# Attention on one core, part of the exponentials on VectorE: the fixed point put into PSUM, a twelfth group for VectorE, and three middle passes on GpSimd

## The chip, the cores and the metric

The kernel runs on one core of a Trainium2 chip. A core has five engines that run side by side, each through its own list of instructions in order, with semaphores between them: TensorE (PE in the profile; its weight loads are PEld), VectorE (DVE), ScalarE (ACT), GpSimd (POOL) and SyncE (SP), which here issues DMAs. SBUF is the working memory of 128 partitions, PSUM the memory that TensorE writes its products to. The metric is the device time of one execution in microseconds (us). Before the change it is 117.99 us, the median of three runs (117.93 to 118.18).

## The reference

```python
def setup_inputs():
    batch, heads, seq, dim = 8, 8, 512, 64
    return {
        "q": np.random.randn(batch, heads, seq, dim).astype(np.float32),
        ...
    }

def reference(q, k, v):
    scale = 1.0 / np.sqrt(q.shape[-1])
    scores = np.einsum('bhqd,bhkd->bhqk', q, k) * scale
    scores = scores - scores.max(axis=-1, keepdims=True)
    attn = np.exp(scores)
    attn = attn / attn.sum(axis=-1, keepdims=True)
    return np.einsum('bhqk,bhkd->bhqd', attn, v).astype(np.float32)
```

This is attention for 64 heads, each of 512 positions of 64 numbers. The kernel leaves out the subtraction of the maximum, which cancels in the quotient.

## The kernel before

The 64 heads are worked off as 32 pairs. For each pair, SyncE loads q, k and v (256 KB each); GpSimd rounds them to 16 bits (`cast`, lines L446 and L456); TensorE transposes q and k into PSUM (`transposes`, L480) and VectorE copies the result to SBUF (`copy`, L493). Then TensorE computes the scores, keys along the partitions. Two blocks of 128 keys by 512 queries make a group of 128 x 1,024 scores that fills one score buffer (tile `st`, L522); there are four groups in a pair, 128 in all, and the very last is done in two halves. A pool of three score buffers is used in strict rotation: group m takes the buffer of group m - 3.

ScalarE takes the exponential of a whole group in one instruction (`pt`, L527) and writes it to SBUF as 16-bit numbers. TensorE then multiplies these weights with v (`values`, L604). v carries an extra column of ones, so that the sum of the weights comes out with the product. VectorE takes the reciprocal of that sum (L582) and multiplies it in (`normalise`, L584), and SyncE stores the finished heads.

Eleven of the groups do not go to ScalarE. They are listed in `ON_DVE`, and VectorE computes their exponential by arithmetic on the bits of a number. TensorE first puts a constant into the score buffer (the `lift` matmuls, L508) and adds the scores. Then VectorE makes four instructions over 1,024 columns: the raise (`raise_`, L544) reads PSUM, multiplies the scores by `STEP` and writes `z`, a number whose upper bits are the exponent and whose lower 16 bits are the fraction. Then come three passes (`pass_`, L561) for a polynomial of that fraction: the first reads the fraction from `z` twice and writes `y`, the middle pass reads `y` twice, and the last reads `y` and `z` and writes the weights `pd`. For the last group of the list (`SHARED = 1`) GpSimd makes the middle pass in two instructions (`middle`, L574 and L577).

The order of all this is fixed before the kernel is built, by the class `Plan`. It steps through time in 5 ns steps with a cost for every kind of instruction (`EXP`, `COPY`, `NORM`, `RAISE`, `PASS`, `CAST`, `MIDDLE`), and decides at each step what TensorE, VectorE, GpSimd and SyncE do next. VectorE prefers copies that the next scores need, then raises, then other work that is ready (`step_dve`); a pass is only started where nothing of more urgency falls due before its end, with tolerances `LATE_NORM` and `LATE_COPY`. The planner keeps `port`, a time until which GpSimd and VectorE's passes exclude each other. `free` tells when the next score buffer can be written, `emit` releases a GpSimd cast, and from the time `CALM` on, each cast is made to wait for the VectorE instruction named last before it (`cast_behind`). Every engine then runs its list in that order, and only semaphores decide the times. The steps `raise`, `pass`, `middle`, `scores` and `last` are those that the change touches, besides the start (`first_pair`), where the first pair is rounded, transposed and scored ahead of the planned part.

Of the kernel before, what the change touches and what calls it, by code (L numbers as in the profile page):

```python
# [17 lines left out]
class Plan:  # L18
# [6 lines left out]
    COPY, NORM, RAISE = (601, 690), (307, 390), (1132, 1215)  # L25
    COPY_1 = (400, 190)
    NORM_COLUMN, PASS_DONE = 67, 80
    PASS, PASSES = 1131, 3
# [3 lines left out]
    CALM, KEEN = 14000, 6  # L32
    FIRST_UNIT = 4
    ON_DVE = (7, 20, 28, 40, 51, 56, 70, 80, 84, 98, 112)
    SHARED = 1

    LATE_NORM, LATE_COPY, HURRY, SOON, BACKLOG = 1000, 2200, 900, 80, 1200
# [7 lines left out]
    def __init__(self, groups, pairs, first):  # L45
# [4 lines left out]
        self.read = []  # L50
        self.exps = {}
        for m in range(first):
            self.act += self.EXP + self.EXP_FIXED
            self.exps[m] = self.act + self.EXP_DONE
            self.read.append(self.exps[m])
# [90 lines left out]

    def free(self, n=0):
        m = self.m + n
        if m >= len(self.groups):
            return 1e9  # L150
        g = self.groups[m][0][0]
        return max(0 if m < 3 else self.read[m - 3], self.tq.get(g, 1e9))
# [4 lines left out]
    def scores(self, t):  # L157
        m, grp = self.m, self.groups[self.m]
        half = m >= len(self.groups) - 2
        slots = 2 if 0 < grp[0][0] and grp[0][2] == grp[1][2] and not half else 1  # L160
        on_dve = self.for_dve(m)
        self.note(t, "scores", m, on_dve)
        t += (0 if self.tiled else self.INTO) + self.SLOT * slots
        self.tiled = True
        if on_dve:
            t += self.OFFSET
            self.ready.append((t + self.TO_DVE, "raise", (m,)))
            self.read.append(1e9)
        else:
            begin = max(self.act, t + self.TO_ACT)  # L170
            self.idle = getattr(self, "idle", 0) + begin - self.act
            self.act = begin + self.EXP // (2 if half else 1) + self.EXP_FIXED
            self.exps[m] = self.act + self.EXP_DONE
            self.read.append(self.exps[m])
        self.m += 1
        self.pe = t
# [35 lines left out]
    def last_values(self, t):  # L212
        g, h = self.last
        if self.m < len(self.groups) or self.last_part == 4:
            return False
        if t < max(self.wants(g, h, self.last_part), self.read[self.last_part // 2 - 3]):
            return False
        self.note(t, "last", self.last_part)
        self.full(t, self.V_UNIT)
        if self.last_part % 2:  # L220
            self.ready.append((self.pe + self.TO_DVE, "finish", (self.last_part // 2,)))
        self.last_part += 1
        return True
# [58 lines left out]
    def step_dve(self, t):  # L282
# [8 lines left out]
        if now:  # L291
# [3 lines left out]
            _, kind, what = job  # L295
            slots = 2 if kind == "raise" else 1
# [7 lines left out]
            if kind == "norm":  # L304
                more = self.NORM_COLUMN * what[1]
                self.dve = t + self.NORM[0] + more
# [5 lines left out]
            elif kind == "copy":  # L312
                held, done = self.COPY if what[0] != 1 else self.COPY_1
                self.dve = t + held
                self.banks[what[1]] = self.tq[what[0]] = t + done + self.TO_PE
            else:
                self.dve = t + self.RAISE[0]
                self.read[what[0]] = t + self.RAISE[1] + self.TO_PE
                self.passes += [(what[0], s, 0) for s in range(self.PASSES)]
            self.dve_done = self.dve  # L320
        elif any(x[2] <= t for x in self.passes):
            m, s, _ = job = next(x for x in self.passes if x[2] <= t)
            end = max(t, self.port) + self.PASS
            late = {"copy": self.LATE_COPY, "norm": self.LATE_NORM, "raise": self.LATE_NORM, "finish": 0}
            if all(x[0] > end - late[x[1]] for x in self.ready):
                self.passes.remove(job)
                self.note(t, "pass", m, s)
                self.dve = self.port = self.dve_done = end
                if s == 0 and m in self.ON_DVE[len(self.ON_DVE) - self.SHARED :]:
                    self.passes.remove((m, 1, 0))  # L330
                    self.passes[self.passes.index((m, 2, 0))] = (m, 2, 1e9)
                    self.casts.append(("middle", m, end + self.TO_POOL))
                    self.note(end, "middle", m)
                if s == self.PASSES - 1:
# [19 lines left out]
def kernel(  # L354
# [12 lines left out]
    scale = float(D) ** -0.5  # L367
    NP = (B * H) // 2
# [22 lines left out]
    ps_st = ctx.enter_context(tc.tile_pool(name="ps_st", bufs=3, space=bass.MemoryType.PSUM))  # L391
# [18 lines left out]
    heads = []  # L410
    raised = {}
# [29 lines left out]

    def cast(g, name):
# [10 lines left out]
        if (g, name) == (1, "q"):  # L453
            nc.vector.tensor_copy(out=dst[:, :, 0:2], in_=src[:, :, 0:2])
            return nc.gpsimd.tensor_copy(out=dst[:, :, 2:4], in_=src[:, :, 2:4])
        return nc.gpsimd.tensor_copy(out=dst, in_=src[:, :, :, :])  # L456
# [41 lines left out]
    def scores(m, on_dve):  # L498
# [3 lines left out]
        st = ps_st.tile([P, 2, S], FP32, tag="st", name=f"st_{m}")  # L502
# [21 lines left out]
        if on_dve:  # L524
# [3 lines left out]
            out=pt[:, :, cols], in_=st[:, :, cols], func=EXP, scale=scale  # L528
# [8 lines left out]
    LIFT, STEP = (793.0 / 32, -0.039907195352 / 32), scale * 1.4426950408889634 * 1024  # L537
    QUARTIC = (7.77974906 * 2.0**16, -8.78105033 * 2.0**32, 4.4655924e-3 * 1024 * 2.0**-64)

    def raise_(m):  # L540
# [6 lines left out]
                scalar1=STEP,  # L547
                scalar2=2.0**17,
                op0=AluOp.mult,
                op1=AluOp.max,  # L550
# [3 lines left out]
    def pass_(m, s):  # L554
        r = raised[m]
        f = r["z"].bitcast(U16).rearrange("p x (s n) -> p x s n", n=2)[:, :, :, 0]
        if s == 0:
# [5 lines left out]
                in0=r["y"][:, :, :] if s else f,  # L563
# [14 lines left out]

    def normalise(u, n):
        o, x = os[u // 7], u % 7  # L580
        rc = opool.tile([P, 7, 1], FP32, tag="rc", name=f"rc_{u}")
        nc.vector.reciprocal(out=rc[:, 0:n], in_=o[:, x : x + n, D : D + 1])  # L582
# [29 lines left out]
    def last_values(part):  # L612
        half, second = divmod(part, 2)
        if not second:
            o = ps_st.tile([P, 2, S], FP32, tag="st", name=f"o_last{half}")
# [39 lines left out]
    def first_pair():  # L655
# [8 lines left out]
        def twice(h, i, n):  # L664
            return tq[:, h, i : i + n].rearrange("p i (x d) -> p i x d", x=1).broadcast_to([P, n, 2, D])

        nc.vector.tensor_copy(out=q16[:, 0, 0:2], in_=twice(0, 0, 2))
        nc.vector.tensor_copy(out=k16[:, 0, 0:2], in_=tk[:, 0, 0:2])
        nc.scalar.copy(q16[:, 0, 2:4], twice(0, 2, 2))
        nc.gpsimd.tensor_copy(out=k16[:, 0, 2:4], in_=tk[:, 0, 2:4])  # L670
        nc.scalar.copy(k16[:, 1], tk[:, 1])
        nc.gpsimd.tensor_copy(out=q16[:, 1], in_=twice(1, 0, NI))

        st0, pka, st1 = (
            ps_st.tile([P, 2, S], FP32, tag="st", name=f"st_{n}") for n in ("0a", "ka", "1")
        )
# [16 lines left out]
        def first_scores(st, h, j, q0, q1, pt, s0, s1):  # L693
            for x in range(2):
# [9 lines left out]
                out=pt[:, :, q0:q1], in_=st[:, :, s0:s1], func=EXP, scale=scale  # L704
# [23 lines left out]
        st0b = ps_st.tile([P, 2, S], FP32, tag="st", name="st_0b")  # L728
# [9 lines left out]
        st2 = ps_st.tile([P, 2, S], FP32, tag="st", name="st_2")  # L738
# [5 lines left out]
    with tc.manual_schedule():  # L744
# [7 lines left out]
        for p in (32, 96):  # L752
            nc.vector.memset(lift[p : p + 32], LIFT[1])
        for n in range(NV):
# [13 lines left out]
            "finish": finish,  # L768
            "norm": lambda u, n, b: normalise(u, n),
        }  # L770
# [32 lines left out]
```

## Time and profile before

| what | us |
|---|---|
| median of three runs | 117.99 |
| lowest, highest | 117.93, 118.18 |
| the profiled execution | 117.88 |
| its span in the trace | 116.1 |

The profile is one execution on the chip. Its page gives each engine's busy time and share of the span; groups of instructions by source line, with the tile written and the tiles read (`pt<-st`), their count, their busy time, the mean duration of one, and the idle time of the engine just ahead of them with what ended it; and the chain of work that ended last. The trace behind it gives windows (busy time of each engine in a stretch) and timelines (instructions in order: start, duration, engine, line). A duration in a timeline runs until the result has landed, so that consecutive instructions of an engine can overlap by about 0.1 us. TensorE's clock was granted in full throughout (0.992 on average), and the DMA engines moved 33.83 MB at 291 GB/s.

### The profile page before, as it was taken

The page shows a single profiled execution, that of the slowest core. Times are in us where ns is not written, and L with a number is a line of the kernel's source. Part 1 is how long each engine was busy: PE and PEld are TensorE (multiplying, and loading weights), DVE is VectorE, ACT ScalarE, POOL GpSimd, SP SyncE. Part 2 cuts the span into 40 slices and gives each one's busy share as a digit, 9 for nine tenths or more (in the row PEclk, how much of TensorE's full clock was granted, in tenths as well). Part 3 has the DMA queues.
Part 4 walks back from the last instruction along what each step waited for, and adds up shares of the span by engine and source line. Part 5 has one row for each costly group of instructions (what it writes and reads, how often), then busy time and mean ns, then how long its engine had stood idle before and what let it go on. Part 6 is the DMA issues. An engine that isn't in the chain of part 4 may idle for free.

```text
span 116.1 us, 4085 instructions
## 1 busy us (share of the span) xinstructions
PE 104.8 (90%) x1581; PEld 66.9 (58%) x1581; DVE 101.4 (87%) x177; ACT 109.7 (95%) x122; POOL 60.5 (52%) x104
## 2 busy tenths in 40 slices
PE   7979989989999999999799979999989999999980
PEld 2635557546676466646465646467845567576660
DVE  3455997699999999999999999999999999969381
ACT  4599999999999999999999999999999999999980
POOL 2378519954653655555425546954484255596000
PEclk9999999999999999999999999999999999999996
DMA  3999999999999999999999999999999994222354
GB/s 109 286 372 380 384 378 384 388 375 375 344 323 319 307 293 336 311 338 307 352 307 305 321 328 241 296 376 324 329 292 358 366 291 167 93 93 93 101 184 133
DMA packets 35604, 33.83 MB, mean 291 GB/s; under 512 B 2688, under 2 KB 35584, under 8 KB 35584
## 3 DMA queue, kind: packets, MB, share of 16 engines
q1 hardware_dynamic: 35152, 33.24, 87.1%
q10 hardware_dynamic: 432, 0.33, 0.9%
q8 instruction: 12, 0.20, 0.7%
q14 instruction: 8, 0.07, 0.2%
HBM read 25.17 MB, written 8.39 MB: 289 GB/s over the span
## 4 chain that ended last, share of the span: by engine, by line
ACT 31%; DVE 30%; PE 18%; DMA 10%; issue 7%; POOL 1%; SPq 0%; POOLq 0%; ACTq 0%
ACT pt L527 29%; DVE y L561 7%; DVE tqk L493 6%; DMA k<-in_k_dram 6%; DVE z L544 6%; PE st L522 6%; PE o L604 6%; DVE ring L584 5%; DMA v<-in_v_dram 4%; DVE pd L561 4%; PE st_0a L653 3%; ACT pt L703 2%; PE tp L480 2%; POOL qkp L456 1%; DVE rc L582 1%
## 5 line engine op out<-in xcount | busy, mean ns | idle before, releaser
L527 ACT ACTIVATE pt<-st 128x1024 f16<-128x1024 f32 (+1 forms) x115 | 104.8, 1216 | 0.0
L522 PE MATMUL st<-tqk 64*128 64x512 f16 (+1 forms) x250 | 44.6, 380 | 4.3 <-ACT pt L527 3.1
L604 PE MATMUL o<-vp,pt 128*128 128x65 f16 x920 | 43.0, 194 | 1.4 <-DVE tqk L493 0.9
L604 PEld LDWEIGHTS <-pt 128*128 128x128 f16 x920 | 36.3, 98 | 11.0 <-issue 9.7
L446 POOL CAST vp<-v 128x512 f16<-128x512 f32 x32 | 19.6, 616 | 18.6 <-DVE y L561 10.9
L456 POOL CAST qkp<-k 128x512 f16<-128x512 f32 x31 | 19.0, 613 | 14.1 <-PE st L522 4.7
L584 DVE TENSOR_TENSOR ring<-o,rc 128x448 f32<-128x448 f32 (+2 forms) x37 | 22.6, 612 | 1.3
L456 POOL CAST qkp<-q 128x512 f16<-128x512 f32 x30 | 18.4, 613 | 10.1 <-DVE y L561 4.8
L522 PEld LDWEIGHTS <-tqk 64*128 64x128 f16 x250 | 13.1, 93 | 17.6 <-issue 10.1
L493 DVE COPY tqk<-tp 128x1024 f16<-128x1024 f16 x30 | 20.3, 683 | 2.3 <-PE tp L480 2.2
L480 PE MATMUL tp<-ident,qkp 128*128 128x128 f16 x248 | 20.5, 220 | 0.6 <-DVE tqk L493 0.2
L480 PEld LDWEIGHTS <-qkp 128*128 128x128 f16 x248 | 14.2, 97 | 8.8 <-issue 4.8
L561 DVE SCALAR_TENSOR_TENSOR pd<-y,z 128x1024 uint32<-128x1024 f32 x11 | 14.2, 1288 | 0.0
L544 DVE TENSOR_SCALAR z<-st 128x1024 f32<-128x1024 f32 x11 | 13.4, 1217 | 0.9 <-PE st L522 0.9
L561 DVE SCALAR_TENSOR_TENSOR y<-z 128x1024 f32<-128x1024 uint16 x11 | 13.9, 1261 | 0.1
L604 PE MATMUL o<-vp,pd 128*128 128x65 f16 x88 | 13.1, 194 | 0.3 <-DVE pd L561 0.2
L561 DVE SCALAR_TENSOR_TENSOR y<-y 128x1024 f32<-128x1024 f32 x10 | 12.3, 1234 | 0.0
L604 PEld LDWEIGHTS <-pd 128*128 128x128 f16 x88 | 8.6, 98 | 3.2 <-issue 2.4
L582 DVE RECIPROCAL rc<-o 128x7 f32<-128x7 f32 (+2 forms) x37 | 7.3, 196 | 3.3 <-PE o L604 3.2
L508 PE MATMUL st<-const-bfloat16-1.0,lift 64*128 64x512 bf16 x22 | 4.3, 381 | 0.4 <-ACT pt L527 0.4
L653 PE MATMUL st_0a<-const-bfloat16-1.0 128*128 128x512 bf16 (+1 forms) x11 | 3.5, 482 | 0.8 <-PEq L787 0.8
L653 PEld LDWEIGHTS <-const-bfloat16-1.0 128*128 128x128 bf16 x15 | 1.7, 129 | 2.5 <-issue 2.4
(50 smaller groups left out, 25.0 us busy)
## 6 DMA issues: line engine op xcount, KB each, us to landing
out_dram<-ring SPq DMA_DIRECT2D x63, 128.0 KB, 3.8
k<-in_k_dram SPq DMA_DIRECT2D x31, 256.0 KB, 5.1
q<-in_q_dram SPq DMA_DIRECT2D x31, 256.0 KB, 5.0
v<-in_v_dram SPq DMA_DIRECT2D x27, 256.0 KB, 5.2
v<-in_v_dram SPq DMA_DIRECT2D x10, 128.0 KB, 4.1
k<-in_k_dram ACTq DMA_DIRECT2D x2, 128.0 KB, 2.9
q<-in_q_dram SPq DMA_DIRECT2D x2, 128.0 KB, 2.7
out_dram<-obl SPq DMA_DIRECT2D x1, 64.0 KB, 1.6
```

What stands on the lines that cost most here:

```text
L446: return nc.gpsimd.tensor_copy(out=vps[g % NV][:, :, :, 0:D], in_=raw[g]["v"][:, :, :, :])
L456: return nc.gpsimd.tensor_copy(out=dst, in_=src[:, :, :, :])
L480: nc.tensor.transpose(tps[g][:, n, i, :], qkp[g][:, n, i, :], ident)
L493: nc.vector.tensor_copy(out=tqk[g][:, :, :], in_=tps.pop(g).rearrange("p n i c -> p n (i c)"))
L522: nc.tensor.matmul(st[:, x, cols], kc, qc[:, cols], start=not on_dve, stop=True)
L527: nc.scalar.activation(out=pt[:, :, cols], in_=st[:, :, cols], func=EXP, scale=scale)
L544: nc.vector.tensor_scalar(out=r["z"][:, :, :], in0=r["st"][:, :, :], scalar1=STEP, scalar2=2.0**17, op0=AluOp.mult, op1=AluOp.max,)
L561: nc.vector.scalar_tensor_tensor(out=r["bits"][:, :, :] if last else r["y"][:, :, :], in0=r["y"][:, :, :] if s else f, scalar=QUARTIC[s], ...
L582: nc.vector.reciprocal(out=rc[:, 0:n], in_=o[:, x : x + n, D : D + 1])
L584: nc.vector.tensor_tensor(out=ring[:, u % NU : u % NU + n, :], in0=o[:, x : x + n, 0:D], in1=rc[:, 0:n].broadcast_to([P, n, D]), op=AluOp. ...
L604: nc.tensor.matmul(os[u // 7][:, u % 7, :], blocks[(g, c, h)][:, y * P : (y + 1) * P], vps[g % NV][:, h, c, :], start=(c == 0), stop=(c == ...
L653: nc.tensor.matmul(dst[:, 0:n], ones[:, 0:P], ones[:, 0:n], start=True, stop=True)
```

## The change

Four things change together.

1. The factor `STEP` is no longer multiplied in by the raise. k is multiplied by 16 and q by `STEP / 16` when they are rounded to 16 bits, so that the score buffer in PSUM holds the fixed-point number itself. The rounding instructions of q and k become multiplications by a constant (`times`), on GpSimd and, in the first pairs, on VectorE and ScalarE. ScalarE's exponentials take `scale / STEP`. The constant that `lift` adds becomes 143 * 1024 - 3/64 per head. The raise keeps only its maximum.
2. The first pass reads the low 16 bits from the score buffer in PSUM and the clamped fraction from `z`, where it read `z` twice. The score buffer is given back after the first pass, not after the raise.
3. The three score buffers become three tiles with a tag each, and the planner takes the one that is free earliest (`pick`), in place of the rotation.
4. `ON_DVE` has twelve groups at other places, and `SHARED` names three of them, 57, 72 and 105, whose middle pass GpSimd makes. The planner's times and tolerances are others; a pass may not start before 117 ns after the one that it depends on; the first pass does not count for `port`, and up to two casts may be released ahead of it. A step that makes the reciprocal apart (`recip`, `mult`) is added and switched off (`APART = False`).

```diff
-    COPY, NORM, RAISE = (601, 690), (307, 390), (1132, 1215)
+    COPY, NORM, RAISE = (601, 690), (307, 390), 1132
...
+    RECIP, RECIP_DONE, CHAINED = 80, 230, 117
+    APART, ROOM = False, 0
...
-    CALM, KEEN = 14000, 6
+    CALM, KEEN = 20000, 6
...
-    ON_DVE = (7, 20, 28, 40, 51, 56, 70, 80, 84, 98, 112)
-    SHARED = 1
-
-    LATE_NORM, LATE_COPY, HURRY, SOON, BACKLOG = 1000, 2200, 900, 80, 1200
+    ON_DVE = (7, 13, 26, 36, 47, 57, 63, 72, 80, 93, 105, 110)
+    SHARED = (57, 72, 105)
+
+    LATE_NORM, LATE_MULT, LATE_COPY, HURRY, SOON, BACKLOG = 1600, 1300, 1400, 800, 80, 1500
...
+    def pick(self):
+        return min(range(3), key=lambda b: self.buffers[b])
+
     def free(self, n=0):
...
-        return max(0 if m < 3 else self.read[m - 3], self.tq.get(g, 1e9))
+        return max(sorted(self.buffers)[n], self.tq.get(g, 1e9))
...
-                self.dve = t + self.RAISE[0]
-                self.read[what[0]] = t + self.RAISE[1] + self.TO_PE
-                self.passes += [(what[0], s, 0) for s in range(self.PASSES)]
+                self.dve = t + self.RAISE
+                self.passes += [(what[0], s, 1e9 if s else self.dve + self.CHAINED) for s in range(self.PASSES)]
...
-            end = max(t, self.port) + self.PASS
+            end = (max(t, self.port) if s else t) + self.PASS
...
+                if s:
+                    self.port = end
+                else:
+                    self.buffers[self.buffer[m]] = end + self.PASS_DONE + self.TO_PE
...
+    STEP = scale * 1.4426950408889634 * 1024
+    TIMES = {"k": 16.0, "q": STEP / 16.0}
...
-    ps_st = ctx.enter_context(tc.tile_pool(name="ps_st", bufs=3, space=bass.MemoryType.PSUM))
+    ps_st = ctx.enter_context(tc.tile_pool(name="ps_st", bufs=1, space=bass.MemoryType.PSUM))
...
+    def times(engine, out, x, name):
+        return engine.tensor_scalar(
+            out=out, in0=x, scalar1=TIMES[name], scalar2=None, op0=AluOp.mult
+        )
...
-        return nc.gpsimd.tensor_copy(out=dst, in_=src[:, :, :, :])
+        return times(nc.gpsimd, dst, src[:, :, :, :], name)
...
+    def buffer(b, name):
+        return ps_st.tile([P, 2, S], FP32, tag=f"st{b}", name=name)
...
-            out=pt[:, :, cols], in_=st[:, :, cols], func=EXP, scale=scale
+            out=pt[:, :, cols], in_=st[:, :, cols], func=EXP, scale=scale / STEP
...
-    LIFT, STEP = (793.0 / 32, -0.039907195352 / 32), scale * 1.4426950408889634 * 1024
+    LIFT = (143.0 * 1024 / 32, 0.0, -3.0 / 64)
...
                 in0=r["st"][:, :, :],
-                scalar1=STEP,
-                scalar2=2.0**17,
-                op0=AluOp.mult,
-                op1=AluOp.max,
+                scalar1=2.0**17,
+                scalar2=None,
+                op0=AluOp.max,
...
-        f = r["z"].bitcast(U16).rearrange("p x (s n) -> p x s n", n=2)[:, :, :, 0]
+        f, low = (
+            r[name].bitcast(U16).rearrange("p x (s n) -> p x s n", n=2)[:, :, :, 0] for name in ("z", "st")
+        )
...
-                in0=r["y"][:, :, :] if s else f,
+                in0=r["y"][:, :, :] if s else low,
...
-        nc.vector.tensor_copy(out=q16[:, 0, 0:2], in_=twice(0, 0, 2))
-        nc.scalar.copy(q16[:, 0, 2:4], twice(0, 2, 2))
+        times(nc.vector, q16[:, 0, 0:2], twice(0, 0, 2), "q")
+        nc.scalar.mul(q16[:, 0, 2:4], twice(0, 2, 2), TIMES["q"])
```

## The prediction

> **What bounds the kernel now.** I read the engines' busy shares first, then the groups by line with their idle time, then the timelines of VectorE (DVE) and GpSimd (POOL), then the chain of waits.
>
> ```profile
> PE 104.8 (90%) x1581; PEld 66.9 (58%) x1581; DVE 101.4 (87%) x177; ACT 109.7 (95%) x122; POOL 60.5 (52%) x104
> ```
> ```profile
> L527 ACT ACTIVATE pt<-st 128x1024 f16<-128x1024 f32 x113 | 103.8, 1225 | 0.0
> ...
> L561 DVE SCALAR_TENSOR_TENSOR pd<-y,z 128x1024 uint32<-128x1024 f32 x11 | 14.2, 1288 | 0.0
> L561 DVE SCALAR_TENSOR_TENSOR y<-z 128x1024 f32<-128x1024 uint16 x11 | 13.9, 1261 | 0.1
> L544 DVE TENSOR_SCALAR z<-st 128x1024 f32<-128x1024 f32 x11 | 13.4, 1217 | 0.9 <-PE st L522 0.9
> ...
> L561 DVE SCALAR_TENSOR_TENSOR y<-y 128x1024 f32<-128x1024 f32 x10 | 12.3, 1234 | 0.0
> ```
> The groups by line give instructions, busy us, mean ns and idle time before them. ScalarE (ACT) has no idle time at all before its 113 full exponentials: 103.8 / 113 = 0.919 us each, end to end. ScalarE sets the time, and one exponential taken from it is worth 0.92 us as long as the next scores are always there. Nothing that only makes another engine faster can show.
>
> The windows, whose columns are length, then busy us of PE, weight loads, DVE, ACT, POOL, then clock and DMA:
> ```profile
> 11.20:100.00 88.80, 83.11 (x1288) 53.84 (x1288) 86.14 (x128) 88.77 (x98) 49.10 (x84) 1.00 0.99 325
> 100.00:112.00 12.00, 11.47 (x208) 7.82 (x204) 8.77 (x17) 12.00 (x14) 5.25 (x6) 1.00 0.30 96
> ```
> DVE is idle 2.66 us up to 100 us and 3.23 us behind it: 5.9 us together. PE is idle 5.7 us in the first of them.
>
> DVE, and then POOL, around the last group that DVE exponentiates:
> ```profile
> 98.34 1.22 DVE L544 TENSOR_SCALAR z<-st 128x1024 f32<-128x1024 f32 x1
> 99.59 1.60 DVE L561 SCALAR_TENSOR_TENSOR y<-z 128x1024 f32<-128x1024 uint16 x1
> 101.11 0.68 DVE L493 COPY tqk<-tp 128x1024 f16<-128x1024 f16 x1
> 101.72 0.19 DVE L582 RECIPROCAL rc<-o 128x7 f32<-128x7 f32 x1
> 101.94 0.62 DVE L584 TENSOR_TENSOR ring<-o,rc 128x448 f32<-128x448 f32 x1
> ...
> 104.86 1.55 DVE L561 SCALAR_TENSOR_TENSOR pd<-y,z 128x1024 uint32<-128x1024 f32 x1
> ```
> ```profile
> 99.50 0.61 POOL L456 CAST qkp<-q 128x512 f16<-128x512 f32 x1
> 101.28 1.04 POOL L574 TENSOR_SCALAR t<-y 128x1024 f32<-128x1024 f32 x1 [1.17 <-DVE y L561]
> 102.41 2.36 POOL L577 TENSOR_TENSOR y<-t,y 128x1024 f32<-128x1024 f32 x1
> 104.71 0.61 POOL L446 CAST vp<-v 128x512 f16<-128x512 f32 x1
> ```
> A pass with both inputs in SBUF is stretched (1.60 and 1.55 against a usual 1.22) where a POOL cast runs; a copy or normalisation reading PSUM is not.
>
> The chain of waits, in order of time, shows a buffer going round:
> ```profile
> 87.68 1.18 ACT pt L527
> 88.86 0.04 issue
> 88.90 0.41 PE st L522 x2
> 89.30 0.02 issue
> 89.34 0.15 issue
> 89.49 1.20 ACT pt L527
> ```
> From the end of an exponential to the start of the next on the refilled buffer: 0.63 us.
>
> **The change, part by part.**
>
> *One group less on ACT:* −0.92 us, all on the path.
>
> *DVE, passes:* 11 raises, 11 first, 10 middle and 11 last passes become 12, 12, 9 and 12: 43 to 45. Back to back one takes 1.13 us (the chain's pieces "DVE z L544" and "DVE y L561"), so +2.3 us. The raise loses its multiplication and stays one instruction from PSUM over 1,024 columns: 0. No row shows a pass with one input in PSUM and one in SBUF, read as every second 16-bit word. Its parts are there: PSUM input (raise, 1,217 ns), two tensors in, one of them every second word (1,261 ns, stretched ones included). Nearest: the raise, so 1.13 us and no change; bounds −0.05 and +0.05 each, 0.6 us in twelve.
> The Trainium skill (Perfetto Trace Analysis, Optimizing Scalar/DVE Operations) gives a DVE instruction about 60 ns of access overhead on SBUF and about 125 on PSUM. By that, twelve passes would cost an estimated 0.8 us more of DVE, still inside its idle time; in this trace raise and pass take the same 1.22 us.
>
> *DVE, the stretching by POOL:* the means of the three pass rows lie above 1,216 ns by 72, 45 and 18, so 11 × 72 + 11 × 45 + 10 × 18 = 1.5 us are lost now. A first pass with only one SBUF input resembles the copies, which were not stretched: −0.5 us. Two more middle passes on POOL let a cast in ahead of the last pass twice more, as at 104.71: 2 × 0.33 = +0.7 us. Together DVE gets +2.5 us, against 5.9 us idle. It fits, but leaves 3.4 us in 101: an engine off the path that is nearly full.
>
> *POOL:* the two middle passes add 2 × (1.04 + 2.36) = 6.8 us to 60.5, covered by its waits for DVE's passes (10.9 + 7.0 + 6.3 + 1.2 us of idle). Its 61 q and k casts become multiplications. Half of L574 is 0.52 us for 512 columns against 0.61 for the cast, but by the step from 128 columns (0.37) to 512 (0.61) one would get about 0.67: −0.09 to +0.06 each. I take 0.
>
> *In each shared group,* the new order has between first and last pass on DVE only copies, normalisations, one raise and one first pass: 5.0, 4.4 and 5.0 us of work over the 3.6 us that the middle pass took (101.19 to 104.77). So the last pass is not what waits, if none of these needs what POOL holds.
>
> *Score buffers:* the buffer of a DVE group is now given back after raise and first pass, not after the raise. By the order of DVE, from the start of the raise to the end of the first pass it is 2 × 1.13 us plus the copies (0.60), normalisations (0.76) and other passes put between: over the twelve groups 2.9, 4.2, 2.9, 2.3, 2.9, 2.3, 2.9, 5.4, 3.6, 2.9, 2.9, 3.6, in sum 39 us against 11 × 1.13 = 12. Behind the score matmuls that wait stand values and transposes on PE; behind them ACT. For these 39 us ACT lives on two buffers, 39 / 0.919 = 42 refills. One refill takes 0.63 us from end to start, and the other buffer's exponential covers it until 0.92 − 0.12 = 0.80 us (0.12 is what the first pair's full exponentials, 1.04 us each, run past their share): 0.17 us to spare. PE's transposes come in eights of about 0.46 to 0.55 us and values in units of about 0.13, so PE has to stand free at the right moment. Taking a free buffer in any order keeps the other two turning while the third is held, where a strict rotation would stop at the third score. Bounds: 0 (ACT is never idle now, though its buffers are short then too) to 42 × 0.03 = 1.3 us. I take +0.1, near the lower, because ACT's row shows 0.0 around eleven such places.
>
> *Start:* q and k of the first pair become multiplications, on DVE ahead of the first transposes. Bounds: the cast's 0.30 and 0.22, or a single-rate row of that width (the 256-column normalisation 0.42, the 128-column one 0.29): 0 to +0.2 us. I take 0, the nearest row being a one-input cast of the same shape. *End:* the last DVE group is 110 in place of 112; the tail behind the last exponential (112.3 to 116.1) is the same work: 0. *PE:* one more pair of lift matmuls, 0.2 us, inside its idle 5.7. *Casts released freely* until 20 instead of 14 us can stretch one or two passes by up to 0.6 us, where DVE has idle time.
>
> Sum against the profiled execution, 117.88 us (span 116.1 and 1.8 around it): 117.88 − 0.92 + 0.10 = 117.06. The median of the three is 0.11 higher, so 117.17.
>
> **The rivals.**
>
> *A, refills come late.* Of 42 two-buffer refills, each late by 0.03 us: +1.3, so 118.3, slower than before. It decides from 0.92 / 42 = 22 ns per refill. For it: the 5.4 us hold of group 72 alone spans six exponentials, and PE is 94% busy; against it: 0.0 idle now. A milder form, 10 ns, gives back half: 117.6; with the whole gain gone it is 118.0.
>
> *B, the first pass still holds what POOL needs.* Then one first pass stands in each shared stretch against a 2.36 us POOL multiplication, and twelve keep losing to casts: 3 × 1.5 to 2.4 plus 0.5 is 5 to 8 us on DVE, beyond the 3.4 left, and what is over goes to ACT: about 118.6 to 121. Against it: PSUM-reading DVE work ran unstretched from 101.1 to 102.6 beside the middle pass. The Trainium skill (SBUF — State Buffer, SBUF: two separate sides) says the pair of ports is locked by a DVE instruction with two SBUF inputs, which speaks against B; the stretched 1.55 us agrees.
>
> *C, multiplications on POOL are dearer than casts.* At +0.15 us each, 61 of them are 9 us, and those hidden under a 0.60 us copy stretch the pass behind: up to 30 × 0.15 = 4.5 us on DVE, 1.1 beyond its idle time: 118.3.
>
> *D, the change does not do what it says:* the 12th group buys 0 because the last group's late end moves PE's last values; then 118.0.
>
> **How the numbers follow.** Forecast (117.0 to 117.4) 0.56; milder A 0.14; gain eaten (A at its threshold, or D) 0.08; A in full 0.12; B 0.05; C 0.05. What 0.2%, 0.24 us, cannot tell from no change counts as the same. Faster 0.70, same 0.08, slower 0.22. Low end: no new stall, and 0.2 of spread between executions, 116.85. High end: to hold 8 in 10 it takes in the milder and full A up to 118.4; B and dearer cases stay out.
>
> **What would show it.** Right: 112 full exponentials with 0.0 to 0.2 us idle; first passes of 1.22 us without stretched ones; q and k multiplications of 0.55 to 0.67 us on POOL; DVE busy near 103 to 104. Wrong: idle time before ACT ended by "PE st", PE waiting for DVE's first pass (A); first passes of 1.5 us and more beside POOL (B); POOL above 76 us busy (C).

## The result and the profile after

| what | us |
|---|---|
| median before, six runs beside the changed kernel | 118.11 (117.93 to 118.89) |
| median after, six runs | 160.73 (158.85 to 161.35) |
| ratio after to before | 1.356, 95% interval 1.350 to 1.361 |
| the profiled execution of after, its span | 161.24, 159.5 |

The changed kernel takes 36% longer: 42.6 us more, where 0.8 us less was forecast, and far outside the forecast's range of 116.85 to 118.4. Ratios here and below leave out runs over 1.5% above the fastest of their kernel; medians, lowest and highest are those of all runs.

The page of the changed kernel, the row of busy times, the granted clock in 40 slices and the chain that ended last by engine:

```profile
PE 120.0 (75%) x1583; PEld 71.8 (45%) x1583; DVE 106.7 (67%) x181; ACT 112.8 (71%) x121; POOL 132.7 (83%) x108
...
PEclk9999959977959978999996599999699999955996
...
POOL 41%; PE 15%; DMA 15%; issue 12%; DVE 12%; SPq 2%; ACT 0%; POOLq 0%; ACTq 0%
```

ScalarE, 95% busy before, is down to 71%, with 112.8 us of work where it had 109.7. GpSimd is the engine that grew: 60.5 us before, 132.7 now, and the chain runs through it. TensorE's clock, granted in full from 4.88 us to the end before, is at half in places.

The groups by line of the changed kernel, different shapes kept apart (instructions, busy us, mean ns, then the idle time just before them and what ended it):

```profile
L577 ACT ACTIVATE pt<-st 128x1024 f16<-128x1024 f32 x112 | 106.7, 1036 | 38.6 <-PE st L572 37.8 <-PE tp L527 0.5
...
L485 POOL TENSOR_SCALAR qkp<-k 128x512 f16<-128x512 f32 x31 | 51.0, 1646 | 4.5 <-DVE ring L641 0.9 <-DMA k<-in_k_dram 0.8 <-PE st L572 0.4
L485 POOL TENSOR_SCALAR qkp<-q 128x512 f16<-128x512 f32 x30 | 48.3, 1609 | 2.4
...
L493 POOL CAST vp<-v 128x512 f16<-128x512 f32 x32 | 19.7, 629 | 3.5 <-DVE y L612 1.9 <-DVE pd L612 0.3
```

The first row is the cost: ScalarE waits 38.6 us ahead of its full exponentials, 37.8 of it for score matmuls. The next three show the reason, which the experiments below confirm. Rounding v is still a cast, 0.63 us for 512 columns. Rounding q and k is now a multiplication over the same shape, and takes 1.61 to 1.65 us. 61 of them are 99.3 us, where the casts were 37.4: 61.9 us more, of the 72.2 us by which GpSimd's work grew. (6.8 more are the two further middle passes. About 1.4 are the shorter multiplications of the first pairs, and about 2 arise in the adding up, since the casts before overlapped one another. By the bare 1.49 us, 61 would take 90.9 us: the other 8.4 of the 99.3 are multiplications that were stretched.)

GpSimd's timeline shows the bare duration and the step from one to the next:

```profile
12.66 1.49 POOL L485 TENSOR_SCALAR qkp<-k 128x512 f16<-128x512 f32 x1
14.23 1.49 POOL L485 TENSOR_SCALAR qkp<-q 128x512 f16<-128x512 f32 x1
15.78 0.61 POOL L493 CAST vp<-v 128x512 f16<-128x512 f32 x1
16.47 1.49 POOL L485 TENSOR_SCALAR qkp<-k 128x512 f16<-128x512 f32 x1
```

1.49 us each, 1.57 from start to start. The planner still reckons with 0.56 (`CAST = 560` is not in the diff), so the order of all engines is laid out for the cast's pace. No run told it the longer one; but GpSimd's 132.7 us of work alone are more than the 118 us that the kernel took before. The waits (us in total, times, longest) say who stands behind:

```profile
PEld L527 <- POOL qkp L485: 40.2, 35, 5.2
ACT pt L577 <- PE st L572: 37.8, 30, 4.8
PE tp L527 <- POOL qkp L485: 30.8, 23, 5.0
```

The transposes and their weight loads wait for the rounded q and k, and with them everything behind them on TensorE, scores included. In its idle stretches TensorE also loses clock: eight times it falls to half, for 3.41 or 6.83 us, the last time until the end of the kernel. The Trainium skill (TensorE: Matmul & The Clock Gate, Part 1: The HAM clock gate) tells of a free-running window of 3,413 ns over which the activity of TensorE is judged; the lengths in this trace agree.

### The profile page after: what moved, and what is told of

The parts are those of the page before. It is cut to its first block, busy times and chain, and to the rows that moved or that the text cites. A ratio compares the mean times of both kernels' runs of the same rounds, so it can differ in the third digit from the quotient of the medians.

```text
span 159.5 us, 4090 instructions
## 1 busy us (share of the span) xinstructions
PE 120.0 (75%) x1583; PEld 71.8 (45%) x1583; DVE 106.7 (67%) x181; ACT 112.8 (71%) x121; POOL 132.7 (83%) x108
## 4 chain that ended last, share of the span: by engine, by line
POOL 41%; PE 15%; DMA 15%; issue 12%; DVE 12%; SPq 2%; ACT 0%; POOLq 0%; ACTq 0%
POOL qkp L485 30%; POOL vp L493 7%; PE o L661 7%; DMA out_dram<-ring 7%; DMA k<-in_k_dram 5%; PE st L572 4%; DVE ring L641 3%; DMA v<-in_v_dram 3%; DVE z L594 3%; PE tp L527 3%; DVE y L612 2%; POOL t L625 2%; DVE tqk L540 2%; POOL y L628 2%; DVE rc L633 1%
## 5 line engine op out<-in xcount | busy, mean ns | idle before, releaser
L577 ACT ACTIVATE pt<-st 128x1024 f16<-128x1024 f32 (+1 forms) x114 | 107.7, 1029 | 38.6 <-PE st L572 37.8
L485 POOL TENSOR_SCALAR qkp<-k 128x512 f16<-128x512 f32 x31 | 51.0, 1646 | 4.5 <-DVE ring L641 0.9
L485 POOL TENSOR_SCALAR qkp<-q 128x512 f16<-128x512 f32 (+1 forms) x31 | 49.1, 1584 | 2.5
L572 PE MATMUL st<-tqk 64*128 64x512 f16 (+1 forms) x250 | 48.5, 417 | 2.6 <-ACT pt L577 1.5
L527 PE MATMUL tp<-ident,qkp 128*128 128x128 f16 x248 | 25.1, 237 | 31.5 <-POOL qkp L485 30.8
L661 PE MATMUL o<-vp,pt 128*128 128x65 f16 x912 | 47.8, 203 | 0.1
L661 PEld LDWEIGHTS <-pt 128*128 128x128 f16 x912 | 39.9, 104 | 16.9 <-issue 16.4
L612 DVE SCALAR_TENSOR_TENSOR pd<-y,z 128x1024 uint32<-128x1024 f32 x12 | 15.9, 1328 | 4.6 <-POOL y L628 4.6
L661 PE MATMUL o<-vp,pd 128*128 128x65 f16 x96 | 16.1, 203 | 0.0
L612 DVE SCALAR_TENSOR_TENSOR y<-st,z 128x1024 f32<-128x1024 uint16 x12 | 14.6, 1215 | 0.1
L612 DVE SCALAR_TENSOR_TENSOR y<-y 128x1024 f32<-128x1024 f32 x9 | 11.5, 1283 | 0.0
L628 POOL TENSOR_TENSOR y<-t,y 128x1024 f32<-128x1024 f32 x3 | 7.0, 2349 | 0.3
```

Source lines behind the costliest of these rows:

```text
L485: return engine.tensor_scalar(out=out, in0=x, scalar1=TIMES[name], scalar2=None, op0=AluOp.mult)
L527: nc.tensor.transpose(tps[g][:, n, i, :], qkp[g][:, n, i, :], ident)
L572: nc.tensor.matmul(st[:, x, cols], kc, qc[:, cols], start=not on_dve, stop=True)
L577: nc.scalar.activation(out=pt[:, :, cols], in_=st[:, :, cols], func=EXP, scale=scale / STEP)
L612: nc.vector.scalar_tensor_tensor(out=r["bits"][:, :, :] if last else r["y"][:, :, :], in0=r["y"][:, :, :] if s else low, scalar=QUARTIC[s] ...
L628: nc.gpsimd.tensor_tensor(out=y[:, :, :], in0=t[:, :, :], in1=y[:, :, :], op=AluOp.mult)
```

## The experiments

**1. Which part of the change costs the time: the multiplications on GpSimd, or the rest?** Four kernels tell it apart. Theory: GpSimd's multiplication with one operation is slow as an instruction, while the row that the prediction priced it from (`t<-y`, L574) has two operations. Rivals: any multiplication is slow there; what GpSimd does is not to blame, but the new order of the passes and score buffers.

The changed kernel with two operations in GpSimd's multiplications, the second by 1.0:

```diff
     def times(engine, out, x, name):
+        if engine is nc.gpsimd:
+            return engine.tensor_scalar(
+                out=out, in0=x, scalar1=TIMES[name], scalar2=1.0, op0=AluOp.mult, op1=AluOp.mult
+            )
```

> The changed kernel with GpSimd's multiplications of q and k in a form with two operations (times the factor, then times 1.0), everything else as it is. Theory 'one operation': GpSimd's slow 1.49 us per 512 columns belongs to the form with a single operation, because the middle pass's two-operation instruction takes 1.04 us for 1,024 columns. Then each takes 0.5 to 0.7 us and the time falls to about 117.2 us. Rival 'rounding': multiplying into 16-bit output is slow on GpSimd whatever the number of operations. Then each stays at 1.4 us or more and the time at about 160 us.

Measured: 122.13 us (121.41 to 123.2), ratio to before 1.033 [1.027, 1.040]. The groups by line:

```profile
L486 POOL TENSOR_SCALAR qkp<-k 128x512 f16<-128x512 f32 x31 | 19.2, 619 | 10.6 <-PE st L576 3.4 <-PE o L665 2.7 <-DMA out_dram<-ring 1.4
```

An operation more in the instruction takes it from 1.65 us to 0.62, and the kernel from 160.7 to 122.1: 38.6 of the 42.6 us.

The changed kernel with plain copies for all rounding, so that the scaling is left out and the weights are those of wrongly scaled scores, with the same work for every engine:

```diff
-        return engine.tensor_scalar(
-            out=out, in0=x, scalar1=TIMES[name], scalar2=None, op0=AluOp.mult
+        return engine.tensor_copy(
+            out=out, in_=x
         )
...
-        nc.scalar.mul(q16[:, 0, 2:4], twice(0, 2, 2), TIMES["q"])
+        nc.scalar.copy(q16[:, 0, 2:4], twice(0, 2, 2))
```

> The changed kernel with all rounding of q and k done by plain copies, as before the change; the scaling is left out altogether, so this computes attention of wrongly scaled scores. Theory 'only GpSimd's multiplications are slow, the rest of the change does what was forecast': 117.2 us (116.85 to 117.5), ScalarE idle below 0.3 us. Rival 'something else in the change costs as well' (score buffers held through the first pass, the first pass on PSUM, three middle passes on GpSimd): 118.0 us or more, with ScalarE waiting for scores.

Measured: 118.44 us (117.86 to 120.39), ratio 1.002 [0.999, 1.005]. Everything else in the change together neither gains nor loses what can be told. That is not the forecast's 117.2 either, so something small remained to be found.

The changed kernel with plain casts, and the scaling by the root of `STEP` in VectorE's copies out of PSUM, which gives the same scores:

```diff
+    ROOT = STEP**0.5
...
+    def scaled(out, in_):
+        return nc.vector.tensor_scalar(out=out, in0=in_, scalar1=ROOT, scalar2=None, op0=AluOp.mult)
...
-            nc.vector.tensor_copy(
+            scaled(
```

> The changed kernel with plain copies for the rounding, and the scaling put into VectorE's copies out of PSUM: each multiplies by the square root of STEP, for q and k alike. It computes the reference. If such a multiplication from PSUM at 16 bits runs as fast as the copy (0.60 us from one to the next), 117.2 us as in the run with plain copies. If it runs at half that speed, 30 x 0.53 = 16 us more on VectorE, which has 3.4 us idle: about 130 us.

Measured: 118.43 us (117.78 to 119.31), ratio 1.003 [0.999, 1.007]. On VectorE the multiplication with one operation costs nothing: the copies out of PSUM keep their mean of 683 ns for 1,024 columns. Again no gain.

The kernel before, with GpSimd's 61 casts as multiplications by 1.0 with one operation and nothing else changed:

```diff
-        return nc.gpsimd.tensor_copy(out=dst, in_=src[:, :, :, :])
+        return nc.gpsimd.tensor_scalar(out=dst, in0=src[:, :, :, :], scalar1=1.0, scalar2=None, op0=AluOp.mult)
```

> The kernel before the change, with GpSimd's 61 full casts of q and k made multiplications by 1.0 in the form with a single operation, and nothing else changed. Theory 'the multiplications are the whole loss': GpSimd gets 61 x 0.9 = 54 us more work on 60.5 us and waits for VectorE's passes besides; about 155 to 165 us. Rival 'they are only slow beside the new order': each takes 0.6 us here and the time stays at 118 us.

Measured: 152.11 us in two runs, ratio 1.286 [1.283, 1.289]. The groups by line:

```profile
L527 ACT ACTIVATE pt<-st 128x1024 f16<-128x1024 f32 x113 | 107.5, 1034 | 30.8 <-PE st L522 30.6
...
L456 POOL TENSOR_SCALAR qkp<-k 128x512 f16<-128x512 f32 x31 | 48.1, 1551 | 5.3 <-DMA k<-in_k_dram 2.7 <-POOL vp L446 1.2 <-PE tp L480 0.6
```

The one edit puts 34 us on the kernel before, with the same wait of ScalarE for scores. So the form of this one instruction is the cause of the slowdown: taken out of the changed kernel (three ways) the loss goes down to 4.0, 0.3 and 0.3 us, put into the kernel before it brings most of the loss with it.

**2. What ate the gain of the twelfth group.** With plain casts the changed kernel should have been 0.8 us faster and was not. In the profiled execution of the kernel with the scaling in the copies, ScalarE idles almost only in the start. Its TensorE timeline there:

```profile
4.74 0.40 PE L754 MATMUL st_0a<-qt,kt 64*128 64x256 f16 x2
5.83 0.40 PE L754 MATMUL st_0b<-qt,kt 64*128 64x256 f16 x2 [0.69 <-ACT pt L761]
5.99 0.66 PE L754 MATMUL st<-qt,kt 64*128 64x512 f16 x2
```

and ScalarE's groups by line:

```profile
L580 ACT ACTIVATE pt<-st 128x1024 f16<-128x1024 f32 x112 | 102.9, 1152 | 0.4 <-PE st L575 0.4
L761 ACT ACTIVATE pt<-st 128x1024 f16<-128x1024 f32 x2 | 2.0, 1020 | 0.8 <-PE st L754 0.8
```

The second half score `st_0b` waits 0.69 us for ScalarE. In the kernel before, the pool's rotation gave it another buffer than `st_0a`, and its matmuls followed at once (4.91 behind 4.73). With a tag for each buffer, the code names buffer 0 for both, so `st_0b` has to wait until ScalarE has read `st_0a`. Behind it on TensorE stand the next scores and the second head's transposes: the copy `qt<-tp_qb` on VectorE starts at 7.18 us in the changed kernel, 5.76 in the one before. And TensorE stays longer at half clock (0.66 us for the two score matmuls against 0.38): full clock comes at 9.9 us in the trace of this kernel, 10.2 in the changed one, 4.9 in the one before. By the fourth full exponential ScalarE is 2.0 us behind (it starts at 10.81 us in the changed kernel and 10.86 here, at about 8.9 with the start mended).

The shared buffer does not bring the slow clock of itself. The kernel with copies has the same wait, and its profile has full clock from 3.45 us on:

```profile
5.26 0.28 PE L751 MATMUL st_0b<-qt,kt 64*128 64x256 f16 x2 [0.69 <-ACT pt L758]
5.37 0.39 PE L751 MATMUL st<-qt,kt 64*128 64x512 f16 x2
```

From the start of its first exponential to that of the fourth full one ScalarE takes 3.68 us in the kernel before, 4.45 with copies and 5.68 here. So about 0.8 us are the buffer's, and the rest of the 2.0 goes with the late clock. Of the four profiles with this wait, full clock comes at 3.45, 9.86, 10.17 and 13.6 us; of the nine without it, at 3.7 to 5.95. Whether the wait makes a late grant likelier, four profiles do not show. Nor is the start the whole of the lost gain everywhere. To see it, take as late what the step from the end of one full exponential to the end of the next exceeds the usual 0.917 us by. In the profile with copies, which took 118.45 us, that sums to 1.29 us, and 0.86 of it fall between 64 and 74 us, behind two passes on VectorE of 1.60 and 1.58 us (at 60.84 and 62.96 us). No run tells whether these two are its cause.

The same kernel with `st_0b` in buffer 2, and the planner told so:

```diff
-            self.exps[m] = self.buffers[m] = self.act + self.EXP_DONE
+            self.exps[m] = self.buffers[2 - m] = self.act + self.EXP_DONE
...
-        st0b = buffer(0, "st_0b")
+        st0b = buffer(2, "st_0b")
...
-        st2 = buffer(2, "st_2")
+        st2 = buffer(0, "st_2")
```

> The run with the scaling in VectorE's copies, and in its start the second half of group 0 scored into the buffer that the first transposed k has left, as in the kernel before the change, and no longer into the buffer that ScalarE is still reading (group 2 then takes that one). Theory 'the start is what the rest of the change loses': TensorE's 0.7 us wait for ScalarE at 5 us is gone, full clock is granted near 4.9 us as before the change, ScalarE's idle time of 2.0 us in the start is gone, 117.1 us (116.8 to 117.4), faster than before by 0.7 to 0.9 us. Rival 'the gain of the twelfth group is lost elsewhere': 117.7 us or more.

Measured: 118.59 us, median of twelve runs (117.13 to 119.41), ratio 0.998 [0.995, 1.002]. The median is no lower than the 118.43 of the start as it was, so over its runs the mended start shows no gain. The profiled execution took 117.4 us (span 115.6). TensorE's timeline:

```profile
4.75 0.40 PE L754 MATMUL st_0a<-qt,kt 64*128 64x256 f16 x2
4.93 0.32 PE L754 MATMUL st_0b<-qt,kt 64*128 64x256 f16 x2
5.09 0.38 PE L754 MATMUL st<-qt,kt 64*128 64x512 f16 x2
```

and ScalarE's groups by line:

```profile
L580 ACT ACTIVATE pt<-st 128x1024 f16<-128x1024 f32 x112 | 102.9, 1174 | 0.0
```

The wait is gone, and in this execution the change is worth what was forecast: 112 exponentials without idle time, the last one ending at 111.88 us where it ended at 112.74 before, 0.86 us earlier. Of that, 0.42 come back behind it: from the last exponential to the end of the span it is 3.74 us, 3.32 before. 0.4 us of it lie behind the landing of the last stores (1.6 us to the end of the span against 1.2); no run tells why.

But the runs are spread: four of the twelve lie at 117.1 to 117.7, eight at 118.2 to 119.4. To see the difference, the same kernel was run again with a profile, twice, and the kernel before once.

> The kernel with the mended start and the scaling in the copies once more, for a second profile: its timed runs lie in two clusters, 117.1 to 117.8 and 118.2 to 119.4 us. Theory 'the start's clock': where the full TensorE clock is granted near 5 us the run takes about 117.4 us, and where it is granted 1.5 us later or more, ScalarE waits in the first 15 us and the run takes 118.5 us or more. Rival 'VectorE and GpSimd meeting by chance': the slower runs have ScalarE waits in the middle, whenever the clock was granted.

> The same kernel a third time, for a third profile, with the same expectations: about 117.4 us with full clock granted near 5 us and no ScalarE waits; 118.5 us or more with either a late grant and ScalarE waits before 15 us (theory of the start's clock), or ScalarE waits in the middle (rival, VectorE and GpSimd).

> The kernel before the change once more, for a second profile. Its runs all lie within 117.6 to 118.9 us but for two outliers. If the time of the clock's grant matters for it as little as that says, a later grant shows less than 0.4 us of ScalarE waits.

Measured: 117.56, 118.39 and 117.86 us. In the 117.56 full clock came at 4.84 us, and the late parts of ScalarE's exponentials sum to 0.22 us, close to the 117.4 (0.13). In the 118.39 it came at 5.91, and TensorE's timeline has:

```profile
4.95 0.42 PE L754 MATMUL st_0b<-qt,kt 64*128 64x256 f16 x2
5.16 0.64 PE L754 MATMUL st<-qt,kt 64*128 64x512 f16 x2
...
8.07 0.87 PE L530 MATMUL tp<-ident,qkp 128*128 128x128 f16 x8 [0.55 <-POOL qkp L485]
```

The matmuls from 5.16 on run at half speed for longer (0.64 against 0.38 us), the next pair's transposes start at 8.07 against 7.06 us, and ScalarE loses 0.25 us at the third and 0.71 at the fifth group, 1.12 us in all: the 1.0 us between the two executions. The larger loss is not the clock's. The transposes wait 0.55 us for GpSimd's cast of k, and that waits for the load of k. GpSimd's timeline in the 118.39, and then in the 117.4:

```profile
7.40 0.62 POOL L485 CAST qkp<-k 128x512 f16<-128x512 f32 x1 [2.89 <-DMA k<-in_k_dram]
```
```profile
5.76 0.61 POOL L485 CAST qkp<-k 128x512 f16<-128x512 f32 x1 [1.17 <-DMA k<-in_k_dram]
```

The kernel with eleven groups of experiment 5 has the same start and tells the two apart: its profile has full clock as late, at 5.95 us, and the cast at 5.27. It loses 0.27 us at the third group and nothing at the fifth. So by these two executions the late clock is worth about 0.25 us, and the 0.71 go with the late load. Why that load landed 1.6 us later, no run tells, and the eight slower ones of the twelve runs have no profile. When full clock is granted differs from run to run. The section of the Trainium skill named above, on the clock gate, says that the moment varies with the phase of the window; these traces agree, at 5.0, 4.8 and 5.9 us in the three profiles of this kernel. Whether the kernel before loses as much when its clock or that load comes late is open: its second profile had the clock early too (5.11 us, 0.16 us of late exponentials).

**3. Do two operations cost as little as a cast?** With them the changed kernel stood at 122.1, not 118.4. Theory: the longer pace, 0.70 us from start to start against the cast's 0.56, lets the plan slip; rival: the rest of it is the start. The two-operation kernel with the start mended as above tells:

> The changed kernel with GpSimd's two-operation multiplications and the same mended start. If the ScalarE waits at 34 and 94 us in the run with two operations came from its late start alone, 117.1 us as with the scaling in the copies. If a two-operation multiplication disturbs VectorE more than a plain cast does, 118 us or more, with those waits still there.

Measured: 121.32 us (121.03 to 122.05), ratio 1.027 [1.023, 1.031]. By the medians the mended start is worth 0.8 us, though the ranges of the two overlap (121.41 to 123.2 without it), and about 3 us remain (3.2 to the kernel before, 2.7 to the mended one with casts). In the profiled execution ScalarE's exponentials fall behind by 4.85 us in all, 3.45 of it at three places of the same kind (1.23, 1.22 and 1.00 us). Around the first, GpSimd's timeline:

```profile
30.60 0.62 POOL L486 TENSOR_SCALAR qkp<-k 128x512 f16<-128x512 f32 x1
31.30 1.58 POOL L486 TENSOR_SCALAR qkp<-q 128x512 f16<-128x512 f32 x1
```

VectorE's:

```profile
31.18 1.22 DVE L616 SCALAR_TENSOR_TENSOR y<-y 128x1024 f32<-128x1024 f32 x1
33.37 0.69 DVE L544 COPY tqk<-tp 128x1024 f16<-128x1024 f16 x1 [0.97 <-PE tp L531]
```

TensorE's:

```profile
32.93 0.40 PE L531 MATMUL tp<-ident,qkp 128*128 128x128 f16 x4 [1.13 <-POOL qkp L486]
```

and ScalarE's, in which five exponentials follow one another after the gap:

```profile
34.14 4.69 ACT L581 ACTIVATE pt<-st 128x1024 f16<-128x1024 f32 x5 [1.12 <-PE st L576]
```

The multiplication of q comes 0.12 us after VectorE's pass has started and is held until it ends: 1.58 us instead of 0.62. The transposes wait 1.13 us for it, the copy 0.97, and ScalarE 1.12. This comes again at 62.27 and 89.65 us (1.65 and 1.68 us). In the mended kernel with casts the pair starts at 29.57 and 30.13 us, and the pass at 30.70, when the second cast is through. So at these three places a pace longer by 0.14 us brings GpSimd to the ports that it shares with VectorE's passes a moment too late. They are 3.45 of the 4.85 us; no run gave the planner the pace of 0.70, which would test it.

**4. Is it the multiplication or the single operation?** In the kernel with the mended start and casts, the first instruction of GpSimd's middle pass, an addition and a multiplication by 1.0 over 1,024 columns, becomes an addition alone, with the same result:

```diff
-            out=t[:, :, :], in0=y[:, :, :], scalar1=QUARTIC[1], scalar2=1.0, op0=AluOp.add, op1=AluOp.mult
+            out=t[:, :, :], in0=y[:, :, :], scalar1=QUARTIC[1], scalar2=None, op0=AluOp.add
```

> The run with the mended start and the scaling in the copies, with the first instruction of GpSimd's middle pass (1,024 columns, 32-bit in and out) in a form with one operation, the addition alone, where it had addition and a multiplication by 1.0. Theory 'every one-operation form on GpSimd is slow, by the column': 2.31 ns a column as in q and k, so 2.5 to 2.7 us instead of 1.04. Rival 'only multiplication, or only 16-bit output, is slow in that form': 1.0 us as before.

Measured, by the groups by line:

```profile
L628 POOL TENSOR_SCALAR t<-y 128x1024 f32<-128x1024 f32 x3 | 8.3, 2770 | 1.5 <-DVE y L615 0.9 <-DVE rc L636 0.6
```

2.77 us against 1.04 with two operations, in 32 bits and with an addition. So the slowness belongs to the form with one operation, not to the multiplication, the rounding or the tile. The kernel took 123.94 us in the one run, 5 to 6 us more than with casts and two operations. How much of that is theirs this run cannot tell: ScalarE is 7.0 us late in it by the end, 1.6 us of that before the first of the three (56.5 us), 1.2 of these behind a stretch in which TensorE's clock was at half (20.7 to 24.1 us). The largest single loss, 2.5 us, comes behind the third (98.0 us).

**5. What is the twelfth group worth?** The mended kernel without group 110 on VectorE, so with 113 full exponentials as before:

```diff
-    ON_DVE = (7, 13, 26, 36, 47, 57, 63, 72, 80, 93, 105, 110)
+    ON_DVE = (7, 13, 26, 36, 47, 57, 63, 72, 80, 93, 105)
```

> The run with the mended start and the scaling in the copies, with eleven groups on VectorE (110 goes to ScalarE). Theory 'ScalarE sets the time, 0.917 us a group': 0.9 us slower than with twelve, so 118.0 us. Rival 'VectorE or the buffers are as near to the limit as ScalarE': within 0.3 us of the run with twelve.

Measured: 119.28 us (118.61 to 120.03), ratio 1.011 [1.006, 1.016].

```profile
L580 ACT ACTIVATE pt<-st 128x1024 f16<-128x1024 f32 x113 | 103.9, 1127 | 0.0
```

ScalarE's last exponential ends at 113.21 us against 111.88 with twelve: 1.33 us, of which 0.40 are more idle time in this execution, and 0.92 the exponential. 0.27 us of that idle time stand in the start, where full clock came at 5.95 us. Against the kernel before, eleven groups in the new arrangement are about 1% slower by these four runs, so the twelfth group does no more than make good what the rest of the change loses.

## Why the prediction was wrong, step by step

**POOL, the step that failed.** "Its 61 q and k casts become multiplications. Half of L574 is 0.52 us for 512 columns … −0.09 to +0.06 each. I take 0." Measured +1.0 us each from start to start (1.57 against 0.56). The row taken as nearest was near in engine, operation name and size, but it has two operations and the new instruction has one. No row before showed a GpSimd instruction of that form, and the bounds were drawn from rows of another form as if the form did not matter. With nothing of its kind in the trace, an end such as the `y<-t,y` row, 2.36 us for 1,024 columns and so 1.18 for 512, belonged in the range. The planner's unchanged `CAST` was not weighed at all. So the multiplications stood in the sum as free, and the waits of TensorE's transposes behind them in no term of it; they account for most of the 42.6 us (38.6 by the two-operation kernel).

**Rival C** named the right instruction, and its sign ("POOL above 76 us busy (C)": it was 132.7), but with +0.15 us each and a chance of 0.05. Where the pace really was 0.14 longer (two operations), the kernel came to 121.3 us, not C's 118.3. C had looked for the loss on VectorE, beyond its idle time; it came through TensorE's transposes, which wait for GpSimd.

**Start**, "0 to +0.2 us. I take 0": the priced instructions did cost nothing (0.29 and 0.22 us on VectorE, multiplication or cast). What was missed stands in the diff as a buffer's number: `st_0b` shares buffer 0 with `st_0a`. By ScalarE's fourth full exponential the changed kernel was 2.0 us behind. With full clock already granted the shared buffer alone cost about 0.8 (the kernel with copies); the rest goes with the late clock, for which the forecast had no term.

**One group less on ACT**, −0.92 us on the path: right where the two faults are out of the way and no load is late: ScalarE's last exponential ends 0.86 us earlier than before in the mended kernel's first profile, with 0.0 us idle, and 0.72 in the second. In the third, with the late load of k, it ends 0.12 us later.

**Score buffers**, +0.1 with A up to +1.3: right at the low end. In the mended kernel's first profile all late exponentials together are 0.13 us, so A is refuted for that execution. For the 0.86 us between 64 and 74 us in the profile with copies, where ScalarE waits for scores (0.34 us at 64.57), it stays open.

**DVE, passes**, first pass from PSUM at no change: right. Line L612 of the changed kernel (ns: least, median, most):

```profile
L612 DVE SCALAR_TENSOR_TENSOR y<-st,z x12: 1206/1214/1224, 16.8 to 135.5; 128x1024 f32<-128x1024 uint16 x12
L612 DVE SCALAR_TENSOR_TENSOR pd<-y,z x12: 1214/1254/1599, 23.8 to 148.3; 128x1024 uint32<-128x1024 f32 x12
```

With GpSimd 83% busy, not one of the twelve first passes was stretched, while last passes with both inputs in SBUF went up to 1.60 us. B is refuted with it. The 125 ns of the Trainium skill (Perfetto Trace Analysis, Optimizing Scalar/DVE Operations) for PSUM against 60 for SBUF do not show: 1,214 ns here against 1,216 from SBUF before. What the Trainium skill says on the locked ports (SBUF — State Buffer, SBUF: two separate sides) agrees.

**DVE as a whole:** forecast 103 to 104 us busy and nearly full; the mended kernel has 102.3. The windows of it (columns as in the prediction):

```profile
11.20:100.00 88.80, 84.51 (x1286) 53.87 (x1284) 87.10 (x130) 88.80 (x98) 61.19 (x91) 1.00 0.98 323
100.00:112.00 12.00, 11.62 (x222) 8.25 (x222) 9.45 (x20) 11.88 (x14) 1.23 (x2) 1.00 0.40 130
```

VectorE is idle 1.70 us up to 100 us, ScalarE not at all: it fits, as forecast, but barely.

**The sum.** With casts and the mended start the kernel took 117.1 to 117.7 us in four of twelve runs, which holds the forecast 117.17; its median is 118.59. So the forecast described the good executions of another kernel than the one that was built. Over its runs the mended kernel cannot be told from the kernel before, and no version here clearly beats it.

## What to carry to other kernels

Price a new instruction from a row of the same form, the number of operations in it included, and by the step from start to start rather than by its duration; where no such row exists, the range has to reach to the dearest row on that engine. When a rotation of buffers is replaced by names, write down for every tile who had its buffer last, the start-up included. A schedule fixed for one pace can turn a small slip into a wait: with 0.14 us more per instruction, on an engine about 60% busy, the kernel was almost 3 us slower here. And one profile of a kernel whose runs spread by 2 us explains that execution only: the slower profile with the mended start lost most of its 1 us behind a load that landed late, the one with copies lost 0.86 us in the middle of the kernel.

## What the runs showed of the hardware that was not expected

- GpSimd's one-operand instruction with a scalar is slow with one operation and fast with two: 1.49 against 0.62 us for 512 columns to 16 bits, 2.77 against 1.04 us for 1,024 columns in 32 bits. With 0.60 us for 128 columns, an estimate from these rows is 2.3 ns a column above a fixed 0.30 us. On VectorE the same form ran at a copy's pace (683 ns for 1,024 columns). The Trainium skill (GPSIMD Engine Reference, 4.1 Engine selection) calls elementwise work with one input on GpSimd "roughly line-rate"; that agrees with the form with two operations and with the cast, and differs from the other by a factor of about 2.5. Why it is so inside the engine, no run shows.
- Two operations have a cast's duration (0.62 against 0.61 us) but a longer pace: 0.70 against 0.56 us from start to start.
- The moment of full clock on TensorE differed between executions of the same kernel, 4.8, 5.0 and 5.9 us with the mended start. In the four profiles where TensorE waits 0.69 us until ScalarE has read `st_0a` it came at 3.45, 9.86, 10.17 and 13.6 us, so the wait alone does not set it; what does, no run shows. A grant at 5.9 us in place of 5.0 cost ScalarE about 0.25 us.
